# Seven block products for eight in a gated MLP

## The chip, the cores and the metric

The kernel runs on one core of a Trainium2 chip. A core has TensorE (PE; matmuls, with the load of the stationary operand shown apart as PEld), VectorE (DVE), ScalarE (ACT), GpSimd (POOL) and SyncE (SP, which issues DMAs here). The metric is device time in microseconds for one execution: the median of three runs.

## The reference

A decoder block over 1024 tokens of width 1024 in float32: a gated-DeltaNet branch and a latent-attention branch, merged by gates and added to the input, then the gated MLP with a causal depthwise convolution of three taps, and a final norm. The change concerns the MLP:

```python
h = rmsnorm(x, norm_ffn_g[l])
u = causal_dwconv(jnp.einsum("bsd,df->bsf", h, w_up[l]), conv_ffn_w[l])
gate_f, up_f = u[..., :D_FF], u[..., D_FF:]
x = x + jnp.einsum("bsf,fd->bsd", jax.nn.silu(gate_f) * up_f, w_down[l])
...
return rmsnorm(x, norm_final_g)
```

D_FF is 2816, that is 22 tiles of 128 features; `w_up` has 2 x 2816 columns (gate and up).

## The kernel before

Every float32 operand of a large product is cut in two fp32r parts, `hi` (a cast on ScalarE) and `lo` (value minus `hi`, on VectorE). A product of two operands is then three matmuls, lo x hi, hi x hi and hi x lo, of 128 x 128 by 128 x 512 into one PSUM bank (`mm3` at L372, `proj_step` at L388).

The parts up to the merge of the branches take the first 1260 us and are not touched. After them `tail` (L1524) projects the merged rows with `w_out`, one token tile at a time (`out_proj`, L1486): the input rows are added (L1506), squared (L1508), scaled by the norm's root and gain (L1512); then TensorE transposes the rows to features (`transpose_rows`, L1514; L1519), and ScalarE and VectorE cut them into `h2` (L1521, L1522). The weights of `out_proj`'s left side are cut at L1494 and L1495. The eight rows of x, 4 MB, stay in SBUF for the rest of the kernel.

`ffn` (L1554) goes over 22 feature tiles. `up(ft)` makes two products, one for gate and one for up: 8 rows of weights x 2 token halves x 3 matmuls each. Each product fills two banks. ScalarE starts the convolution out of PSUM (L1574), VectorE does the other two taps (L1577), ScalarE the silu (L1580), GpSimd the product of gate and up (L1584; the last tile's on VectorE), and the activation is cut at L1585 and L1586. Weights come in through `load_w` (L349; the cuts are L355 and L356). After every two tiles `down` multiplies the two activations of the tiles before with their rows of `w_down` for 8 token tiles x 2 halves (L1600, matmuls at L375 to L377), and VectorE adds each bank to x (L1601). The last four tiles' down-products are interleaved with the final norm (L1629 to L1655). The activations never leave SBUF.

The order of the instructions on each engine is that of the program in `tail` and `ffn`; in the last part, and in all parts before the merge, it is written out by a planner (`Flow`, L170): threads yield instructions with an estimated time, and the most urgent that is ready goes first. Its times are constants such as `0.07 + 0.00104 * n` us for VectorE (L138). On the chip each engine takes its queue in that order and waits on semaphores where data is not ready.

Of the kernel before, what the change touches and what calls it, by code (L numbers as in the profile page):

```python
# [8 lines left out]
F32 = mybir.dt.float32  # L9
# [60 lines left out]
class Memory:  # L70
    """SBUF in KB per partition: regions of one type at a time, and in them the places of tiles, by name."""
# [57 lines left out]
def mm(n, fn):  # L129
    """A float32 product with n columns."""  # L130
    return "pe", 0.0017 * n, fn, None
# [18 lines left out]
def sp(us, fn):  # L150
    """A load that takes the memory for this time."""
# [110 lines left out]
class Block:  # L262
# [27 lines left out]
    def small_constants(self, flow):  # L290
        """Matrices and per-channel vectors; rows of 128 channels turn into columns on the tensor engine."""
# [38 lines left out]
    def bank(self, tag, *shape):  # L330
        """The next PSUM tile of a ring; two banks for "mm"."""
# [17 lines left out]
    def load_w(self, src, kt, n, keep=None):  # L349
        """Streams a weight block [P, kt, n] and splits it exactly into two fp32r parts."""  # L350
# [11 lines left out]
    def rstd(self, ss, n, name):  # L362
        """(ss / n + eps) ** -0.5 for a small [P, m] tile."""
# [24 lines left out]
    def proj_step(self, ps, w, r, k, n):  # L388
        """The k-th of the n terms of a product in two banks."""
# [10 lines left out]
    def mix_in(self, flow, hT):  # L400
# [9 lines left out]
        def mean_root(ss, n, name):  # L410
            """(ss / n + eps) ** -0.5."""
# [141 lines left out]
    def decays(self, flow, ab):  # L553
        """Per-token log decay (softplus without overflow or cancellation), its sums in a chunk, beta."""
# [55 lines left out]
    def load_steps(self, flow, n, src):  # L610
        """Weights of job n: their load, then their split into two parts."""
# [15 lines left out]
    def gdn_conv(self, ps, n, out=None, acc=None):  # L627
        """Of one head's projected q, k or v by feature: causal convolution over time, silu."""
# [13 lines left out]
    def gdn_decay(self, flow, h, pre):  # L642
        """Decays from one token of a chunk to a later one, as exponentials of sums; zero to an earlier one."""
# [21 lines left out]
    def gdn_prepare(self, flow, h, kq, pre):  # L665
        """Key norms and score matrices of every chunk, values by token."""
# [75 lines left out]
    def gdn_blocks(self, flow, h, ma):  # L742
        """Inverses of the diagonal blocks of I + M by forward substitution, half of a block's columns per partition, on M^T's blocks."""
# [37 lines left out]
    def gdn_inverse(self, flow, h, ma, pre):  # L781
        """Transposed inverse of the unit lower triangle I + M of every chunk: pairs of blocks merge,
# [938 lines left out]
```

## Time and profile before

| | |
|---|---|
| median of three runs | 2082.28 us (2081.77 to 2082.43) |
| span of the profiled execution, first to last instruction | 2080.7 us |
| TensorE busy | 2064.0 us, 99% |
| VectorE busy | 1200.3 us, 58% |
| ScalarE busy | 790.0 us, 38% |
| GpSimd busy | 245.8 us, 12% |
| DMA | 142.13 MB, mean 68 GB/s |
| MLP | from 1350 us to the end |

The profile is of one execution; its span lies 1.6 us under the median of the runs, the work around the first and last instruction. Busy time of TensorE includes pipelined matmuls that overlap, so the mean length of one matmul (395 ns) is not its price; the distance from one to the next is. Busy shares are averages over all stages.

### The profile page before, as it was taken

The numbers are of one execution on the slowest core, as the hardware profiler recorded it, in microseconds if no ns is written. First come the engines' busy times: TensorE is split into PE (matmuls) and PEld (weight loads), VectorE is DVE, ScalarE is ACT, GpSimd is POOL, SyncE is SP. The second block draws the span as 40 slices with busy tenths as digits, with TensorE's granted clock in tenths as the row PEclk, the third lists the DMA queues.
The fourth block names the chain that finished last, engine by engine and source line by source line (L and its number), as shares of the span: only waits on it lengthen the run. The fifth ranks groups of instructions, "written<-read, shape, count | busy, mean of one in ns | idle before, by whom it ended". The sixth has DMA issues, their size and how long they took to land.

```text
span 2080.7 us, 27905 instructions
## 1 busy us (share of the span) xinstructions
PE 2064.0 (99%) x11037; PEld 1730.2 (83%) x11037; DVE 1200.3 (58%) x2355; ACT 790.0 (38%) x1698; POOL 245.8 (12%) x230
## 2 busy tenths in 40 slices
PE   9999999999999999999999999999999999999998
PEld 8987888888888888888888888888888888888887
DVE  7377678778788635666674223345354543445436
ACT  5275365366354435554462112232221222222223
POOL 3132021022020002020000031001000000000000
PEclk9999999999999999999999999999999999999999
DMA  6122212212212341111127343012111111111112
GB/s 209 46 60 64 77 39 63 68 48 54 77 49 54 107 133 31 32 37 34 46 90 225 121 134 110 1 56 67 51 51 41 49 53 51 51 38 47 58 31 82
DMA packets 183896, 142.13 MB, mean 68 GB/s; under 512 B 42410, under 2 KB 165012, under 8 KB 183764
## 3 DMA queue, kind: packets, MB, share of 16 engines
q1 hardware_dynamic: 174756, 120.60, 19.9%
q10 hardware_dynamic: 7056, 12.65, 1.7%
q0 software_dynamic: 1952, 7.08, 1.0%
q8 instruction: 87, 1.43, 0.3%
q14 instruction: 45, 0.37, 0.1%
HBM read 114.36 MB, written 25.95 MB: 67 GB/s over the span
## 4 chain that ended last, share of the span: by engine, by line
PE 95%; DVE 2%; DMA 1%; ACT 1%; issue 0%; SPq 0%; POOLq 0%; POOL 0%; ACTq 0%
PE psum L392 54%; PE psum L375 6%; PE psum L377 6%; PE psum L376 6%; PE psum L1395 5%; PE psum L490 3%; PE psum L1404 3%; PE psum L1349 1%; PE psum L1501 1%; PE psum L1504 1%; PE psum L1503 1%; PE psum L680 1%; PE psum L872 1%; PE psum L906 1%; PE psum L916 1%; PE psum L874 1%
## 5 line engine op out<-in xcount | busy, mean ns | idle before, releaser
L392 PE MATMUL psum<-ht,w 128*128 128x512 f32 x4800 | 1171.0, 395 | 1.0 <-ACT ht L1418 0.7
L392 PEld LDWEIGHTS psum<-ht,w 128*128 128x128 f32 x4800 | 881.7, 188 | 172.7 <-ACT ht L1418 1.3
L1577 DVE SCALAR_TENSOR_TENSOR s<-psum,cols,s 128x1023 f32<-128x1023 f32 x88 | 112.6, 1279 | 234.5 <-ACT s L1574 234.5
L1574 ACT ACTIVATE s<-psum,cols 128x1024 f32<-128x1024 f32 x44 | 49.1, 1117 | 212.4 <-PE psum L392 212.4
L375 PE MATMUL psum<-s,s 128*128 128x512 f32 x320 | 124.5, 389 | 0.0
L376 PE MATMUL psum<-s,s 128*128 128x512 f32 x320 | 124.5, 389 | 0.0
L377 PE MATMUL psum<-s,s 128*128 128x512 f32 x320 | 124.5, 389 | 0.0
L1584 POOL TENSOR_TENSOR s<-s 128x1024 f32<-128x1024 f32 x21 | 50.3, 2396 | 611.5 <-DVE s L1577 611.5
L637 DVE SCALAR_TENSOR_TENSOR s<-psum,cols,s 128x511 f32<-128x511 f32 (+1 forms) x144 | 105.2, 739 | 5.0 <-ACT s L632 4.8
L767 DVE TENSOR_TENSOR s<-sc,s 64x240 f32<-64x240 f32 (+27 forms) x248 | 85.3, 344 | 5.3 <-DMA sc<-md_dram 0.7
L769 DVE TENSOR_TENSOR s<-s 64x240 f32<-64x240 f32 (+27 forms) x248 | 80.9, 326 | 6.0
L1601 DVE TENSOR_TENSOR s<-s,psum 128x512 f32<-128x512 f32 x72 | 49.5, 687 | 48.2 <-PE psum L377 48.2
L1329 DVE TENSOR_REDUCE nm<-psum 128x1 f32<-128x256 f32 (+5 forms) x64 | 48.3, 756 | 41.6 <-PE psum L1396 41.6
L624 DVE TENSOR_TENSOR w<-raw,w 128x512 fp32r<-128x512 f32 x96 | 65.5, 686 | 10.5 <-ACT w L622 10.4
L376 PEld LDWEIGHTS psum<-s,s 128*128 128x128 f32 x320 | 60.1, 188 | 12.5
L377 PEld LDWEIGHTS psum<-s,s 128*128 128x128 f32 x320 | 60.1, 188 | 12.5
L375 PEld LDWEIGHTS psum<-s,s 128*128 128x128 f32 x320 | 60.1, 188 | 12.4
L355 ACT CAST s<-raw 128x1024 fp32r<-128x1024 f32 x20 | 21.0, 1051 | 129.8 <-PE psum L376 116.7
L392 PE MATMUL psum<-s,w 128*128 128x512 f32 x288 | 69.8, 391 | 0.0
L490 PE MATMUL psum<-s,ht 128*128 128x400 f32 (+1 forms) x384 | 69.7, 336 | 0.0
L1395 PE MATMUL psum<-ht 128*128 128x384 f32 (+5 forms) x288 | 65.0, 352 | 0.1
L1585 ACT CAST s<-s 128x1024 fp32r<-128x1024 f32 x22 | 23.1, 1051 | 110.4 <-POOL s L1584 106.4
(377 smaller groups left out, 3332.1 us busy)
## 6 DMA issues: line engine op xcount, KB each, us to landing
raw<-in_w_in_dram SPq DMA_DIRECT2D x48, 512.0 KB, 4.5
raw<-in_w_up_dram SPq DMA_DIRECT2D x23, 512.0 KB, 3.9
rx<-in_w_up_dram SPq DMA_DIRECT2D x21, 512.0 KB, 3.9
raw<-in_w_down_dram SPq DMA_DIRECT2D x21, 512.0 KB, 3.6
sg_dram<-s ACTq DMA_DIRECT2D x16, 512.0 KB, 2.7
s<-sg_dram SPq DMA_DIRECT2D x16, 512.0 KB, 3.6
s<-in_x_dram SPq DMA_DIRECT2D x12, 512.0 KB, 6.2
oa_dram<-s POOLq DMA_DIRECT2D x8, 512.0 KB, 3.1
```

The costliest lines, as they stand in the source:

```text
L375: self.nc.tensor.matmul(ps, lhsT=ll, rhs=rh, start=first, stop=False)
L376: self.nc.tensor.matmul(ps, lhsT=lh, rhs=rh, start=False, stop=False)
L377: self.nc.tensor.matmul(ps, lhsT=lh, rhs=rl, start=False, stop=last)
L392: product = lambda o, l, r, **kw: pe(0.2155, lambda: self.nc.tensor.matmul(o, lhsT=l[:, k, :], rhs=r, **kw))
L490: yield pe(0.000417 * (b - a), lambda: tensor.matmul(ps[:, u, :b - a], lhsT=l[:, k, cs], rhs=w[:, k, a:b], start=n == 0, stop=n == 3 * KD ...
L624: yield dve(512, lambda: nc.vector.tensor_tensor(out=lo[:, c], in0=raw[:, c], in1=f(hi[:, c]), op=ALU.subtract))
L637: yield dve(570, lambda: nc.vector.scalar_tensor_tensor(out=o, in0=src[:, max(a - d, 0):b - d], scalar=self.cw[:, n, j:j + 1], in1=o, op0= ...
L767: yield dve(n * w, lambda: nc.vector.tensor_tensor(out=t, in0=mb[:, j, j + 1:].unsqueeze(2).to_broadcast(sh), in1=xb[:, j, :w].unsqueeze(1 ...
L769: yield dve(n * w, lambda: nc.vector.tensor_tensor(out=xb[:, j + 1:, :w], in0=xb[:, j + 1:, :w], in1=t, op=ALU.subtract))
L1395: nc.tensor.matmul(ps[:, n, :w], lhsT=l, rhs=r[:, n * w:(n + 1) * w], start=t == 0, stop=t == len(terms) - 1 and n != parts - 1)
L1404: self.nc.tensor.matmul(po[:, q0:], lhsT=x[:, j, :], rhs=y[:, j, q0:], start=x is vl and j == 0, stop=y is ptl and j == b)
L1577: nc.vector.scalar_tensor_tensor(out=acc[:, d:], in0=src[:, :S - d], scalar=self.cf[:, n, j:j + 1], in1=acc[:, d:], op0=ALU.mult, op1=ALU.add)
```

## The change

Both products of the MLP are done by Strassen's scheme in Winograd's form. An operand is a 2 x 2 matrix of blocks; seven products p1 to p7 of blocks and of sums of blocks take the place of eight, and the sums cost additions on the other engines.

Up: the 2 x 2 blocks are gate and up columns against two halves of the 8 weight rows, and the two token halves. The token side's sums are made once, in `rows_out`, out of the transposed rows (t1 to t4); the rows of x go to DRAM as soon as they are known. The weight side's four sums of each tile are made by GpSimd (`sums`). A pair of gate and up tile then uses four PSUM banks; p1 is copied to a second bank (`seed`), p7 to SBUF (`copy`), and two additions on PSUM (`third`, `fourth`) combine partial results in the middle of the matmuls. The convolution, silu and gate product are as before, but the activation goes to DRAM.

Down: a stage of its own after all 22 tiles. It takes the tiles in three groups of 2m (m = 3, 4, 4). Blocks of activations (L) and of `w_down` (R) are read from DRAM; GpSimd makes four sums of L blocks and VectorE four of R blocks; ScalarE and VectorE cut the operands of each product; the products go to PSUM banks 0 to 3 and 4 to 7 in turns, one more copy (`seed`) shares p1, and VectorE adds banks into the reloaded x. The projection, the up stage and the down stage are all in one plan of `Flow`, so that stages overlap where places in SBUF come free.

```diff
-    def mm3(self, ps, l, r, first, last):
-        nc = self.nc
+    def mm3(self, ps, l, r, first, last, **kw):
         (lh, ll), (rh, rl) = l, r
-        self.nc.tensor.matmul(ps, lhsT=ll, rhs=rh, start=first, stop=False)
-        self.nc.tensor.matmul(ps, lhsT=lh, rhs=rh, start=False, stop=False)
-        self.nc.tensor.matmul(ps, lhsT=lh, rhs=rl, start=False, stop=last)
+        self.nc.tensor.matmul(ps, lhsT=ll, rhs=rh, start=first, stop=False, **kw)
+        self.nc.tensor.matmul(ps, lhsT=lh, rhs=rh, start=False, stop=False, **kw)
+        self.nc.tensor.matmul(ps, lhsT=lh, rhs=rl, start=False, stop=last, **kw)
...
+        def row(s, b, ps):
...
+            yield dve(1150, lambda: vector.tensor_tensor(out=t, in0=y, in1=t, op=ALU.add))
+            ss = self.rowstat[:, s, 0:1]
+            yield act(1150, lambda: scalar.activation(out=y, in_=t, func=AF.Square, accum_out=ss))
...
+            r = yield from self.mean_root(s, D)
...
+            yield dma(lambda: nc.sync.dma_start(out=self.x2_dram[s], in_=t))
+            yield LOAD
+            flow.give("x", x)
+            flow.post(("stored", s))
+            if s == order[-1]:
+                flow.give("wraw", 3)
+            if all(("stored", n) in flow.when for n in range(NS)):
+                flow.give("sums", 0)
...
+        def turned(j):
+            c, c2 = slice(j * P, (j + 1) * P), slice(512 + j * P, 512 + (j + 1) * P)
+            if j:
+                yield On(("first sum", j - 1), ("sums", j - 1), ("h", j - 1))
+            p11 = yield from turn(j, 0, 3)
...
+            flow.post(("left", j))
+            p12 = yield from turn(j + 4, 0, 4)
...
+            yield act(512, lambda: scalar.copy(out=t1, in_=p12))
+            flow.post(("turned", j))
+            yield sub(t3, p22, t1)
+            yield sub(t1, t1, p11)
+            flow.post(("first sum", j))
+            flow.fork(halves_of("t1", t1, c, j), 0.8)
+            yield sub(t2, p22, t1)
+            yield sub(t4, p21, t2)
+            flow.post(("sums", j))
+            yield from halves("h", p22, c)
+            flow.post(("h", j))
...
+        def rest(name, half, at):
+            (hi,), (lo,) = h2[name]
+            yield On("projected")
+            for j in range(4):
...
+                c, src = slice(j * P, j * P + P), mg[half][:, :, at + j * P:at + j * P + P]
+                yield act(512, lambda: scalar.copy(out=hi[:, :, c], in_=src))
...
+        def sums():
+            for ft in range(NF):
...
+                yield Get("sums")
+                g, u = raws[ft, 0][1], raws[ft, 1][1]
+                t = self.m("sums", P, 4, 4, P)
+                lo, hi = slice(0, 4), slice(4, 8)
+                for n, x, y, op in ((0, u[:, lo], u[:, hi], ALU.add), (1, t[:, 0], g[:, lo], ALU.subtract),
+                                    (2, g[:, lo], u[:, lo], ALU.subtract), (3, g[:, hi], t[:, 1], ALU.subtract)):
+                    yield pool(1.2, lambda: nc.gpsimd.tensor_tensor(out=t[:, n], in0=x, in1=y, op=op))
+                raws[ft] = t
+                flow.post(("wsums", ft))
...
+                x = yield Get("wop")
+                both = self.m(f"wop{x}", P, 2, 4, P, dt=F32R)
+                hi, lo = both[:, 0], both[:, 1]
+                yield act(512, lambda: scalar.copy(out=hi, in_=src))
+                yield dve(512, lambda: vector.tensor_tensor(out=lo, in0=src, in1=f(hi), op=ALU.subtract))
...
+                if name == "p3":
+                    flow.give("sums", 0)
+                    for part in range(2):
+                        flow.give("wraw", raws[ft, part][0])
...
+        def pair(ft):
+            a = 4 * (ft % 2)
+            c, d, e = a + 1, a + 2, a + 3
...
+            free = {0: {"a": ["projected", ("h", 2), ("op", 3)], "e": [("first sum", 3)], "d": []},
+                    1: {"a": [("turned", 3), ("op", 7)], "e": [("sums", 3)], "d": ["marked"]}}.get(ft, dict(a=[("evicted", ft - 2)], e=[], d=[]))
+            yield On(*free["a"])
+            def seed():
+                yield act(540, lambda: scalar.copy(out=bank(c), in_=bank(a)))
+                flow.post(("seed", ft))
+            def add(out, event):
+                yield On(("copied", ft), *free["d"])
+                yield dve(620, lambda: vector.tensor_tensor(out=bank(out), in0=bank(c), in1=p7, op=ALU.add))
+                flow.post((event, ft))
...
+            def copy():
+                yield On(("operand", "t1"), ("operand", "t2"))
+                yield act(540, lambda: scalar.copy(out=p7, in_=bank(e)))
+                flow.post(("copied", ft))
...
+            yield from term(ft, "p1", a, True)
+            flow.fork(seed(), 2)
+            if ft < 2:
+                yield On(("seed", ft))
+                yield from term(ft, "p2", a, False)
+            for name in ("p6", "p7") if ft < 2 else ("p7", "p6"):
+                if name == "p7":
+                    yield On(*free["e"])
+                    yield from term(ft, "p7", e, True)
+                    p7 = self.m("p7", P, 512)
+                    flow.fork(copy(), 2)
+                else:
+                    yield On(("seed", ft))
+                    yield from term(ft, "p6", c, False)
+                    flow.post(("summed", ft))
+            flow.fork(add(d, "third"), 2)
+            if ft > 1:
+                yield On(("seed", ft))
+                yield from term(ft, "p2", a, False)
+            yield On(("third", ft))
+            yield from term(ft, "p5", c, False)
+            flow.fork(add(e, "fourth"), 2)
+            yield from term(ft, "p4", d, False)
+            yield On(("fourth", ft))
+            yield from term(ft, "p3", c, False)
+            flow.fork(evict(ft, a), 3)
+        def evict(ft, a):
...
-            nc.scalar.activation(out=us[0], in_=us[0], func=AF.Silu)
-            ah = self.m("a_hi", P, S, dt=F32R)
-            al = self.m("a_lo", P, S, dt=F32R)
-            eng = nc.vector if ft == NF - 1 else nc.gpsimd
-            eng.tensor_tensor(out=us[0], in0=us[0], in1=us[1], op=ALU.mult)
...
+        nc, i = self.nc, self.i
+        tensor, scalar, vector = nc.tensor, nc.scalar, nc.vector
+        places = dict(blk={n: at for n, at in enumerate((194, 0, 186, 114, 98, 146, 154, 162, 170, 178, 12, 20))},
+                      lop=dict(enumerate((66, 34))), rop=dict(enumerate((50, 82))))
...
+        groups, f0 = [], 0
+        for m in (3, 4, 4):
+            groups.append((f0, f0 + m, m))
...
+        def free():
+            yield On(("acts", 1))
+            flow.give("blk", 0)
+            last_ft = NF - 1
+            yield On(("w", last_ft, "p3"))
...
+            flow.give("blk", 9)
+            yield On(("fourth", last_ft))
+            flow.give("blk", 2)
...
+            yield On(("p5", last_ft))
+            self.m.open(F32, "sb")
...
+            yield On(("p3", last_ft))
+            self.m.open(F32, "s2", "s3", "w", "s1", "sc", "sd")
+            for n in (5, 6, 10, 11):
+                flow.give("blk", n)
+            flow.post("x2 places")
+            yield On(("acts", last_ft))
...
+        def loads():
+            for n, (fa, fb, m) in enumerate(groups):
+                for name in ("L11", "R11", "L12", "R21", "L21", "L22", "R12", "R22"):
+                    x, t = yield from block(n)
+                    row, col = int(name[1]) - 1, int(name[2]) - 1
+                    f1 = (fa, fb)[col if name[0] == "L" else row]
...
+        def combine(n, side):
...
+                else:
+                    step = dve(512 * m, lambda: vector.tensor_tensor(out=o, in0=a, in1=b, op=kind))
+                yield step
+                blocks[n, to] = out
...
+                s1 = yield from block(n)
+                yield from op(s1, blk("L21"), blk("L22"), ALU.add, "S1")
+                yield On(("cut", n, "L11"))
+                yield from op(blk("L21"), blk("L11"), blk("L21"), ALU.subtract, "S3")
+                yield from op(blk("L11"), s1, blk("L11"), ALU.subtract, "S2")
+                yield On(("cut", n, "L12"))
+                yield from op(blk("L12"), blk("L12"), blk("S2"), ALU.subtract, "S4")
+            else:
+                yield On(("block", n, "R12"), ("block", n, "R22"))
+                t3 = yield from block(n)
+                yield from op(t3, blk("R22"), blk("R12"), ALU.subtract, "T3")
+                yield On(("cut", n, "R11"))
+                yield from op(blk("R12"), blk("R12"), blk("R11"), ALU.subtract, "T1")
+                yield from op(blk("R11"), blk("R22"), blk("T1"), ALU.subtract, "T2")
+                yield On(("cut", n, "R21"))
+                yield from op(blk("R21"), blk("R21"), blk("T2"), ALU.subtract, "T4")
+        factors = dict(p1=("L11", "R11"), p2=("L12", "R21"), p6=("S2", "T2"), p7=("S3", "T3"), p5=("S1", "T1"), p4=("L22", "T4"), p3=("S4", "R22"))
...
+        def cuts(side):
+            for n, (_, _, m) in enumerate(groups):
+                for p in order:
+                    name = factors[p][side]
+                    x = yield Get(("lop", "rop")[side])
+                    both = self.m(f"{('lop', 'rop')[side]}{x}", P, 2, 4, 512, dt=F32R)
+                    yield On(("block", n, name))
...
+                    for k0 in range(0, m, 2):
+                        ks = slice(k0, min(k0 + 2, m))
+                        w = 512 * (ks.stop - ks.start)
+                        yield act(w, lambda: scalar.copy(out=both[:, 0, ks], in_=src[:, ks]))
+                        yield dve(w, lambda: vector.tensor_tensor(out=both[:, 1, ks], in0=src[:, ks], in1=f(both[:, 0, ks]), op=ALU.subtract))
+                    ops[n, p, side] = x, both
...
+        def products():
+            for n, (_, _, m) in enumerate(groups):
+                for p in order:
+                    yield On(("op", n, p, 0), ("op", n, p, 1))
+                    (xl, l), (xr, r) = (ops.pop((n, p, side)) for side in range(2))
+                    base = 4 if p in ("p6", "p5", "p3") else 0
+                    before = dict(p1=("p4", n - 1), p2=("seed", n), p6=("seed", n), p7=("p2", n), p5=("p6", n), p4=("p7", n), p3=("p5", n))[p]
+                    for j in range(4):
+                        if p == "p1" and n == 0:
...
+                            for k in range(m):
+                                cs = slice(j * P, (j + 1) * P)
+                                self.mm3(ps, (l[:, 0, k, cs], l[:, 1, k, cs]), (r[:, 0, k], r[:, 1, k]), p in ("p1", "p7") and k == 0, k == m - 1,
+                                         skip_group_check=p not in ("p1", "p7"))
...
+                        if p == "p1":
+                            flow.fork(seed(n, j), 2)
+                        else:
+                            flow.fork(add(n, p, j), 2)
+                    flow.give("lop", xl)
+                    flow.give("rop", xr)
...
+        def seed(n, j):
+            yield On(("used", "p3", n - 1, j) if n else ("evicted", NF - 1))
+            yield act(540, lambda: scalar.copy(out=self.psum[:, 4 + j, :], in_=self.psum[:, j, :]))
...
+        def add(n, p, j):
+            s, half, base = dict(p2=(j, 0, 0), p6=(j + 4, 0, 4), p7=(j + 4, 1, 0), p5=(j + 4, 1, 4), p4=(j + 4, 0, 0), p3=(j, 1, 4))[p]
+            yield On(("x2", s))
+            o = x2[s][:, halves[half]]
+            yield dve(600, lambda: vector.tensor_tensor(out=o, in0=o, in1=self.psum[:, base + j, :], op=ALU.add))
+            flow.post(("used", p, n, j))
```

The token tiles are projected in the order 0, 4, 1, 5, 2, 6, 3, 7. In the up stage `order` is p1, p7, p6, p2, p5, p4, p3 from the third tile on.

## Rows read from the trace of the kernel before

**Rows 1.** The page of the profile, its head: span, engines' busy time, instructions

```profile
span 2080.7 us, 27905 instructions
...
PE 2064.0 (99%) x11037; PEld 1730.2 (83%) x11037; DVE 1200.3 (58%) x2355; ACT 790.0 (38%) x1698; POOL 245.8 (12%) x230
...
```

**Rows 2.** The chain of waits, 1240 us to the end: start, length, engine, line

```profile
...
1464.09 43.52 PE psum L392 x192
...
2073.14 0.24 PE psum L377
...
```

**Rows 3.** Busy time by window; PE, PEld, DVE, ACT, POOL, clock, DMA, GB/s

```profile
...
1464.09:1529.37 65.28, 65.28 (x289) 54.07 (x289) 30.26 (x32) 14.53 (x15) 4.79 (x2) 1.00 0.16 49
...
```

**Rows 4.** Who waited for whom, TensorE, 1354 us to the end

```profile
...
PE psum L1519 <- DVE s L1512: 0.5, 1, 0.5
```

**Rows 5.** Groups by line and shape, 1230 us to the end

```profile
...
L1577 DVE SCALAR_TENSOR_TENSOR s<-psum,cols,s 128x1023 f32<-128x1023 f32 x44 | 56.5, 1283 | 234.5 <-ACT s L1574 234.5
...
L1584 POOL TENSOR_TENSOR s<-s 128x1024 f32<-128x1024 f32 x21 | 50.3, 2396 | 611.5 <-DVE s L1577 611.5
L1601 DVE TENSOR_TENSOR s<-s,psum 128x512 f32<-128x512 f32 x72 | 49.5, 687 | 48.2 <-PE psum L377 48.2
...
L356 DVE TENSOR_TENSOR w<-rx,w 128x1024 fp32r<-128x1024 f32 x23 | 28.0, 1216 | 0.0
...
L355 ACT CAST s<-raw 128x1024 fp32r<-128x1024 f32 x20 | 21.0, 1051 | 129.8 <-PE psum L376 116.7 <-DMA raw<-in_w_down_dram 13.1
...
L1495 DVE TENSOR_TENSOR w<-s,w 128x512 fp32r<-128x512 f32 x16 | 11.0, 688 | 18.9 <-ACT w L1494 18.9
L1494 ACT CAST w<-s 128x512 fp32r<-128x512 f32 x16 | 9.9, 621 | 68.6 <-PE psum L1504 55.7 <-POOL s L1484 8.5 <-PE psum L392 4.4
...
L1521 ACT CAST ht<-psum 128x512 fp32r<-128x512 f32 x16 | 9.3, 583 | 6.2 <-PE psum L1519 5.9
...
```

**Rows 6.** Timelines of GpSimd and VectorE in two places: start, length

```profile
...
1446.73 2.40 POOL L1584 TENSOR_TENSOR s<-s 128x1024 f32<-128x1024 f32 x1 [18.84 <-DVE s L1577]
1447.10 1.40 DVE L1601 TENSOR_TENSOR sd<-sd,psum 128x512 f32<-128x512 f32 x2
1448.41 1.81 DVE L356 TENSOR_TENSOR w<-raw,w 128x1024 fp32r<-128x1024 f32 x1
...
1968.97 2.40 POOL L1584 TENSOR_TENSOR s<-s 128x1024 f32<-128x1024 f32 x1 [18.83 <-DVE s L1577]
1970.65 1.80 DVE L356 TENSOR_TENSOR w<-raw,w 128x1024 fp32r<-128x1024 f32 x1
...
```

**Rows 7.** The chain of waits after the last projection product, 1349 to 1356 us

```profile
...
1349.60 0.24 PE psum L1504
...
1354.42 0.66 PE psum L1519 x4
...
```

**Rows 8.** Timeline of TensorE at the start of the kernel

```profile
...
7.54 1.27 PE L469 MATMUL psum<-ident,sc 128*128 128x128 f32 x8 [0.70 <-issue]
11.54 1.09 PE L469 MATMUL psum<-ident,sd 128*128 128x128 f32 x4 [2.72 <-ACT ht L473]
...
```

**Rows 9.** Windows of 1 us: length, TensorE busy, granted clock, DMA, GB/s

```profile
...
10.00:11.00 1.00, 0.00 (x0) 0.64 1.04 415
11.00:12.00 1.00, 0.46 (x3) 0.50 1.04 415
...
16.00:17.00 1.00, 1.00 (x5) 0.50 1.02 406
17.00:18.00 1.00, 1.00 (x8) 0.95 1.03 394
...
```

**Rows 10.** DMA issues on the page: size, us from issue to landing

```profile
...
raw<-in_w_up_dram SPq DMA_DIRECT2D x23, 512.0 KB, 3.9
...
raw<-in_w_down_dram SPq DMA_DIRECT2D x21, 512.0 KB, 3.6
sg_dram<-s ACTq DMA_DIRECT2D x16, 512.0 KB, 2.7
...
```

More of the change, by code (lines that the diff above doesn't have):

```diff
@@ L1548, in tail @@
[L1548 to L1565 removed]
+        self.back(mg, w_out, gb)
@@ new lines, in mean_root, with back @@
+    def mean_root(self, s, n):
+        nc = self.nc
+        ss, ms, r = (self.rowstat[:, s, k:k + 1] for k in (0, 2, 3))
+        yield dve(1, lambda: nc.vector.tensor_scalar(out=ms, in0=ss, scalar1=1.0 / n, scalar2=EPS, op0=ALU.mult, op1=ALU.add))
+        yield pool(0.47, lambda: nc.gpsimd.tensor_tensor(out=r, in0=ms, in1=self.mhalf[:, :1], op=ALU.pow))
+        return r
+    def back(self, mg, w_out, gain):
+        for names in (dict(x0=178, x1=182), dict(wraw0=0, wraw1=4, wraw2=8, wraw3=28), dict(sums=178, p7=ring(186, 2, 2)),
+                      {f"wop{n}": at for n, at in enumerate((12, 16, 20, 24, 130, 134, 138, 142))},
+                      {f"u{n}": 162 + 4 * n for n in range(4)}, dict(mh0=20, mh1=22, ml0=24, ml1=26)):
+            self.m.place(**names)
+        self.rowstat = self.small.tile([P, NS, 4], F32, name="rowstat", bufs=1)
+        self.x2_dram = self.dram.tile([NS, P, D], F32, name="x2_dram")
+        self.act_dram = self.dram.tile([NF, P, S], F32, name="act_dram")
+        flow = Flow(op=(1, 5), x=(0, 1), wraw=(0, 1, 2), wop=(0, 1), sums=(), u=(), blk=(), lop=(), rop=())
+        with self.tc.manual_schedule(engines=self.engines):
+            h2 = self.rows_out(flow, mg, w_out, gain)
+            self.ffn_up(flow, h2)
+            self.ffn_down(flow)
+            flow.run()
@@ L1595, in down @@
-        def down(group):
-            ws = {ft: self.load_w_down(ft) for ft in group}
-            for s in range(NS):
-                for ns in halves:
-                    ps = self.bank("dn")
-                    add_product(ps, s, ns, ws, group, True, True)
-                    nc.vector.tensor_tensor(out=x2[s][:, ns], in0=x2[s][:, ns], in1=ps, op=ALU.add)
-        for n, group in enumerate(groups):
-            for ft in group:
-                up(ft)
-            if 0 < n < len(groups) - 1:
-                down(groups[n - 1])
@@ new lines, in mark, with emit, pairs @@
+        def mark():
+            yield On(("h", 3))
+            def emit():
+                for n in range(4):
+                    tensor.matmul(self.psum[:, 6, n * P:(n + 1) * P], lhsT=self.identb, rhs=self.identb, start=n == 0, stop=True,
+                                  skip_group_check=True)
+            yield pe(0.24, emit)
+            flow.post("marked")
+        def pairs():
+            for ft in range(NF):
+                flow.fork(pair(ft), 10 + ft)
+            yield 0.0
+        for steps, rank in ((loads(), 4), (sums(), 4), (splits(), 4), (mark(), 1), (pairs(), 0)):
+            flow.fork(steps, rank)
@@ L1655, in scaled, with sides, finishes @@
             flow.post(("out", s, n))
-        def tiles():
-            for s in range(NS):
-                flow.fork(tile(s), s)
-            yield 8.5
-            flow.post("acts")
-        with self.tc.manual_schedule(engines=self.engines):
-            flow.fork(tiles(), 0)
-            flow.run()
-    def load_w_down(self, ft):
-        hi, lo = (self.m(n, P, 1, D, dt=F32R) for n in ("dhi", "dlo"))
-        return self.load_w(self.i["w_down"][0, ft * P:(ft + 1) * P, :].unsqueeze(1), 1, D, keep=(hi, lo))
+        def sides():
+            for n in range(len(groups)):
+                for side in "LR":
+                    flow.fork(combine(n, side), 5 + n)
+            yield 0.0
+        def finishes():
+            yield On(("used", "p7", last, 3))
+            for s in (4, 5, 6, 7, 0, 1, 2, 3):
+                flow.fork(finish(s), 2.5)
+        for steps, rank in ((free(), 0), (residual(), 3), (loads(), 6), (sides(), 0), (cuts(0), 5), (cuts(1), 5), (products(), 50), (finishes(), 0)):
+            flow.fork(steps, rank)
     def run(self):
```

395 lines of the change are left out of this document (284 added, 111 removed).

## The prediction

> **What bounds the kernel now.** I read the page first: TensorE is busy 99% of a span of 2080.7 us, VectorE 58%, ScalarE 38%, GpSimd 12% [rows 1]. A busy TensorE need not be at its pace, so next the chain of waits through the MLP: it is made of L392 (up) and L375 to L377 (down) alone, and a stretch of 192 up-products takes 43.52 us, 0.2267 us each [rows 2]. The windows view of one period, two up-tiles and one down-group, gives 192 + 96 = 288 products in 65.28 us, 0.2267 us again, with TensorE never idle and VectorE busy 30.26 of it [rows 3]. So both kinds of product have one price, and nothing else is on the path. The list of waits confirms it: from 1354 us to the end TensorE waited once, for 0.5 us [rows 4]. Whatever takes products away saves 0.2267 us each, as long as the other engines still deliver in time; every new wait of TensorE is paid in full, because there is no slack in it now.
>
> **Removed.** Up: 22 tiles x 2 parts x 8 rows of weights x 2 halves x 3 products = 2112. Down: 22 x 16 x 3 = 1056. After: up 22 x 7 blocks x 4 x 3 = 1848; down 7 blocks x 4 x 3 x (3+4+4) = 924. 396 products fewer, x 0.2267 = **89.8 us**. The 64 transposes stay; four small products of `mark` (0.24 us by the planner's entry) are nothing.
>
> **The load on the other engines, up.** A pair (one up-tile, both parts) is 84 products, 19.04 us. VectorE: 7 weight cuts at 0.69 (L1495), 4 convolution steps at 1.28 (L1577), 2 PSUM additions at 0.69 (nearest row L1601): 11.3 us [rows 5]. GpSimd: the gate product 2.40 and 4 weight sums of half its size at 1.20: 7.2 us [rows 5]. ScalarE has 7 casts of 0.62 and 2 PSUM copies of 0.58 [rows 5] beside what it does today. All fit, so on sums alone the pair is TensorE's. The hand-overs inside it are the new waits: p5 waits for `third` (copy of p7, then an addition), p3 for `fourth`. Each is covered by one block of 12 products, 2.72 us; it needs 0.69 plus two hand-overs of some 0.2 (estimate), so 1.6 us are to spare, more than one convolution step (1.28) in front. I take 0.1 us a pair, **2 us**; the ends are 0 and the slower rival below.
>
> **Down.** A group of m=4 is 336 products, 76.2 us; m=3, 57.1 us; together 209.5. VectorE in m=4: 28 cuts of 1024 at 1.22 (L356), 4 R-sums of 2048 at 2.4 (twice that), 24 additions at 0.69: 60.4 us. GpSimd: 4 L-sums at 4.8 (twice L1584): 19.2. In m=3: 14 cuts at 1.22, 14 at 0.69, 4 sums at 1.83, 24 additions: 50.6; GpSimd 14.4 [rows 5]. VectorE alone fits. But the timeline shows that the two do not run side by side. GpSimd runs 1446.73 to 1449.13; two VectorE additions that read PSUM take their usual 0.69 each meanwhile, and the cut that starts at 1448.41 takes 1.81 instead of 1.22, ending 1.1 after GpSimd. Of nine such cuts in the MLP these are the first and the last [rows 6]; each starts while a GpSimd product runs. So a VectorE instruction with two SBUF inputs waits until GpSimd has finished. By that, cuts and sums (43.9) and GpSimd (19.2) exclude each other, and with the additions (16.5) fill 79.6 us against 76.2; for m=3 50.6 + 14.4 = 65.0 against 57.1. Over all groups 224.2 - 209.5 = 14.7 us is the bound if nothing overlaps, 0 if the additions and VectorE's idle fifth always stand against GpSimd. They do so in part, since VectorE takes its queue in order: **5 us**, a third. The planner that writes the queues has no entry for such a block, so it cannot order around it.
>
> The Trainium skill (SBUF — State Buffer, section SBUF: two separate sides) has this as a rule: VectorE and GpSimd share a pair of ports under an exclusive lock, and a VectorE instruction with two SBUF inputs blocks fully against one of GpSimd. The trace agrees (1.81 against 1.22 us). By it the down groups give back up to 14.7 us; by the sum of each engine's own work, nothing.
>
> **Front: from the output projection to full pace, 9 us.** Today the last row's chain, from the last projection product to its first transposes, takes 4.8 us [rows 7], covered by up-products on the other half. After, all sums of token halves need the last row. Cover: p1, p2 of tile 0 (5.4 us), then of tile 1. For the first two tiles p2 goes into p1's bank and waits for the seed copy (0.58 and two hand-overs): 1.0 us twice. Tile 0's p6 needs weight sums, whose place is free only when the last row is stored: row done at some 6.2 (the 4.8 and its second half, an estimate), store 2.7 [rows 10], four sums 4.8, cast and cut 1.3, hand-overs 0.7: 15.7 us after the projection, 18.5 if each sum waits out one cut of 0.69. TensorE has work to 13.8 (48 products 10.9, two quads of transposes 0.9, the two seed waits). So 1.9 to 4.7, taken 2.8. In both tiles p5 follows p7 directly: copy 0.58, addition 0.69, three hand-overs, 1.9 twice. Tile 1's sums wait for tile 0's p3 cut: 0 to 1, taken 0.5. Sum 9.1; ends 4 (planner fills some) and 15.
>
> **Middle: last pair to first down group, 8 us.** The buffers of p1's operands open at `fourth` of the last tile, 4.5 us before its end (p4 and p3 less 0.95). Four cuts 3.8 plus a first cast 1.05: 0.6 us late. p6 needs R12, R22, loaded only when the last product is done: 768 KB each at 3.6 us per 512 KB [rows 10], landed about 7 us on; then three R-sums 5.5. VectorE also owes the last tile's convolutions 5.1, the cuts of p2 and p6 7.6 and three additions 2.1: 20.3 in all, against p1 and p2's 16.3 us. Late by 4; by 17 if GpSimd's three L-sums and the gate product (13.2) all exclude it. Convolutions and additions (7.2) can run against GpSimd, which leaves 10 at most. Between 4 and 10 I take 7.4, and 0.6 for p1. DMA: 22 activation stores, 8 stores and reloads of x2, the L reads and w_down in blocks, all on SP's queue; transfers of 2.7 to 3.9 us [rows 10] against waits of tens, hidden except where named.
>
> **Clock.** After the gap that ends at 11.54 us [rows 8] the granted clock is 0.64 and then 0.50, back to 0.95 in the window at 17 us [rows 9]: 1.2 GHz for some 6.4 us, 3.2 lost. Gaps of 0.5 us cost nothing [rows 4]. Two stalls above are of that length: **6 us**, between 0 and 13 (four).
>
> The Trainium skill (TensorE: Matmul & The Clock Gate, section Why this matters for your kernels) also warns that idle gaps between bursts of matmuls throttle the clock; the rows show it at the start of this kernel.
>
> **Tail.** Last product to last store as today; VectorE has nothing to cut in the last block: **1 us**, 0 to 3.
>
> **Sum.** 2080.7 - 89.8 + 9 + 2 + 8 + 5 + 6 + 1 = 2021.9 of span. The median, 2082.28, is 1.6 over the span; so 2023.5 us. What this kernel's measurement can tell from no change is 0.2%, about 4 us.
>
> **Rivals.**
> *Nothing is lost beyond some 15 us* (GpSimd stands against additions and idle time, the clock stays up): front and middle at their lower ends and 2 for the rest, 2082.3 - 89.8 + 4 + 4 + 2 = 2002.5; up to 2008 counts here. For it: VectorE alone needs 79% of a group, and waits are covered by whole blocks. Against: rows 6. 0.20.
> *VectorE and GpSimd become the bound of down and its entry*: groups 14.7, middle 17, front 15, clock 13, up 5, tail 3: 68 given back, 2060; anything over 2045 counts here. For it: 79.6 us of VectorE and GpSimd in a group of 76.2, and 65.0 in 57.1. 0.14.
> *Slower: the PSUM additions are on the path in every pair.* Place: `third` and `fourth`, 44 hand-overs. Price: a convolution step 1.28, then a cut with the gate product in front, 0.69 + 2.40, addition 0.69, hand-overs 0.4: 5.5, less 2.72 cover, 2.7 each, 119 us; with the front and middle 2082.3 - 89.8 + 119 + 17 = 2128. It decides from 1.6 us each, (89.8 - 17) / 44. Against: VectorE is busy 11.3 of 19.04 us, and the gate product comes after the convolutions, when `third` is through. 0.03.
> *No gain, the pace per product rising to 0.26*: both kinds run at 0.2267 whatever the operands [rows 2, 3]. 0.01, within 0.2%.
>
> My forecast, 30 us given back, 2008 to 2045: 0.62. The range leaves out half of the best case's lower part and most of the worst: 1999 to 2052. Faster 0.96, same 0.01, slower 0.03.
>
> **What would show it.** 1848 and 924 products of the MLP at 0.2267 us. TensorE idle in pairs 2 to 21 under 3 us in all; some 10 us idle within 40 us after the projection and 8 after the last pair, with a granted clock below 1 behind one or two of them; cuts of 1.22 drawn out to 3 us or more while GpSimd sums; waits of TensorE for VectorE cuts at p6 of each group. I am wrong if pairs take clearly over 19.1 us, if the down groups take their 209.5 us with GpSimd's sums beside VectorE's cuts at full pace, or if the path leaves TensorE for DMA.

## The result and the profile after

The changed kernel takes **2032.18 us** in the median (2030.94 to 2034.51, 4 runs) against 2082.03 (2081.52 to 2082.43, 4 runs) for the kernel before: a ratio of 0.9767 [0.9753, 0.9781]. The forecast was 2023.5 in a range of 1999 to 2052: the sign and the range held, and the forecast was 8.7 us low. Of the 89.8 us removed, 40.4 come back (2031.3 of span against 2080.7), where the sum had 31. They came back in the stages where the prediction looked for them, but not always at the block it named.

The head of the page after, for [rows 1]:

```profile
span 2031.3 us, 27793 instructions
...
PE 1987.2 (98%) x10645; PEld 1660.7 (82%) x10645; DVE 1410.7 (69%) x2504; ACT 896.5 (44%) x1920; POOL 443.4 (22%) x331
...
PE 89%; DVE 6%; DMA 1%; ACT 1%; issue 1%; POOL 0%; SPq 0%; POOLq 0%; ACTq 0%; DVEq 0%
```

TensorE has 392 instructions less: 396 products gone, `mark`'s four added. The last line is the chain that ended last, over the whole span. The same line of the page before:

```profile
PE 95%; DVE 2%; DMA 1%; ACT 1%; issue 0%; SPq 0%; POOLq 0%; POOL 0%; ACTq 0%
```

VectorE's part of the chain has grown from 2% to 6%. Next the windows view of pairs 2 to 21, and of 20 us at the entry of the down stage, in the columns of [rows 3]:

```profile
1398.54:1787.78 389.24, 389.24 (x1717) 322.32 (x1718) 300.19 (x266) 164.37 (x245) 168.29 (x97) 1.00 0.27 86
1790.00:1810.00 20.00, 12.72 (x48) 9.86 (x47) 20.00 (x10) 6.57 (x9) 17.57 (x5) 0.78 0.87 339
```

In the pairs TensorE is busy in every one of 389.24 us, at the full clock. At the entry of the down stage it works 12.72 of 20 us, at 0.78 of its clock, while VectorE is busy throughout with ten instructions and GpSimd for 17.57 with five. The list of TensorE's waits from 1353 us on, for [rows 4] (total, times, longest):

```profile
PE psum L376 <- DVE ht L2013: 12.4, 5, 6.6
PE psum L374 <- ACT ht L2012: 4.0, 2, 3.7
PE psum L374 <- ACT psum L1796: 3.3, 2, 2.6
PE psum L374 <- DVE psum L1801: 2.8, 2, 1.4
PE psum L1637 <- DVE s L1618: 2.0, 1, 2.0
PE psum L374 <- DVE w L1768: 1.4, 1, 1.4
PE psum L374 <- DVE s L1768: 0.4, 1, 0.4
```

L2012 and L2013 are the casts and cuts of the down operands: 16.4 us. The other five rows, 9.9 us, lie in the first two up-tiles. TensorE's timeline says which block each of the longest was in (the wait stands at the end):

```profile
1358.63 0.50 PE L374 MATMUL psum<-ht,w 128*128 128x512 f32 x1 [2.63 <-ACT psum L1796]
1363.48 0.66 PE L1637 MATMUL psum<-ident,s 128*128 128x128 f32 x4 [2.00 <-DVE s L1618]
...
1805.95 0.80 PE L376 MATMUL psum<-ht 128*128 128x512 f32 x1 [6.60 <-DVE ht L2013]
1818.84 0.77 PE L374 MATMUL psum<-ht 128*128 128x512 f32 x1 [3.66 <-ACT ht L2012]
...
1870.56 0.80 PE L376 MATMUL psum<-ht 128*128 128x512 f32 x1 [3.05 <-DVE ht L2013]
```

In order, TensorE waited there for the seed before p2 of tile 0, the scale of row 7, the cut of **p2** of the first group (its third product needs the lower part), the cast of p6, and the cut of p1 of the second group. A smaller wait for a cut, 1.62 us at 1849.10, is in p4 of the first group. What VectorE and GpSimd did around the longest, for [rows 6]:

```profile
1791.98 5.12 DVE L2013 TENSOR_TENSOR ht<-s,ht 128x512 fp32r<-128x512 f32 x2
1797.03 1.27 DVE L1846 SCALAR_TENSOR_TENSOR s<-psum,cols,s 128x1023 f32<-128x1023 f32 x1
1798.22 3.84 DVE L1972 TENSOR_TENSOR w<-w,s 128x1536 f32<-128x1536 f32 x1
1801.98 1.27 DVE L1846 SCALAR_TENSOR_TENSOR s<-psum,cols,s 128x1022 f32<-128x1022 f32 x1
1803.17 2.72 DVE L2013 TENSOR_TENSOR ht<-s,ht 128x512 fp32r<-128x512 f32 x1
...
1792.20 3.83 POOL L1970 TENSOR_TENSOR s<-sb,s 128x1536 f32<-128x1536 f32 x1 [12.38 <-DMA s<-act_dram]
1796.10 4.34 POOL L1970 TENSOR_TENSOR sb<-s,sb 128x1536 f32<-128x1536 f32 x1
1800.52 8.70 POOL L1970 TENSOR_TENSOR s<-s,s 128x1536 f32<-128x1536 f32 x2
```

The first row takes two cuts of different size together. The view of line L2013 from 1790 to 1800 us keeps them apart (shortest, median and longest in ns):

```profile
L2013 DVE TENSOR_TENSOR ht<-s,ht x2: 684/2604/4525, 1792.0 to 1792.6; 128x512 fp32r<-128x512 f32 x1, 128x1024 fp32r<-128x1024 f32 x1
```

While GpSimd sums (L1970), a cut of 1024 columns takes 4.53 us in place of 1.22, a sum 3.84 in place of 1.74 and p2's last cut 2.72 in place of 0.69, 7.4 us of stretching; the cut of 512 that began ahead of GpSimd keeps its 0.68, and the convolution steps (L1846), which read PSUM, keep their 1.27. Last the windows of 1 us, for [rows 9]:

```profile
1367.00:1368.00 1.00, 1.00 (x4) 0.77 (x3) 1.00 (x2) 0.32 (x1) 0.00 (x0) 0.50 0.78 229
...
1807.00:1808.00 1.00, 1.00 (x4) 0.81 (x3) 1.00 (x1) 0.00 (x0) 1.00 (x1) 0.50 0.07 29
1822.00:1823.00 1.00, 1.00 (x4) 0.81 (x3) 1.00 (x2) 0.00 (x0) 0.00 (x0) 0.50 0.41 23
1872.00:1873.00 1.00, 1.00 (x4) 0.80 (x3) 1.00 (x1) 0.33 (x1) 0.00 (x0) 0.50 0.00 0
```

The clock fell four times, each time around one of these waits. Busy time times missing clock, summed over the windows of each fall, is 2.7 (front), 2.8, 2.9 and 2.9 us: 11.3. With the waits, 26.35 from 1353 us on and 1.1 in the projection, that makes 38.8 us, or 38.3 without the 0.5 that TensorE waited there before, of the 40.4; the rest is less than two runs of the kernel differ by.

### The profile page after: what moved, and what is told of

Same layout as the page of the kernel before. It is cut to its first block, busy times and chain, and to the rows that moved or that the text cites. A ratio compares the mean times of both kernels' runs of the same rounds, so it can differ in the third digit from the quotient of the medians.

```text
span 2031.3 us, 27793 instructions
## 1 busy us (share of the span) xinstructions
PE 1987.2 (98%) x10645; PEld 1660.7 (82%) x10645; DVE 1410.7 (69%) x2504; ACT 896.5 (44%) x1920; POOL 443.4 (22%) x331
## 3 DMA queue, kind: packets, MB, share of 16 engines
q8 instruction: 84, 1.38, 0.3%
## 4 chain that ended last, share of the span: by engine, by line
PE 89%; DVE 6%; DMA 1%; ACT 1%; issue 1%; POOL 0%; SPq 0%; POOLq 0%; ACTq 0%; DVEq 0%
PE psum L391 32%; PE psum L374 11%; PE psum L376 11%; PE psum L375 11%; PE psum L1394 5%; PE psum L489 3%; PE psum L1403 3%; DVE ht L2013 2%; PE psum L1348 2%; PE psum L1568 1%; PE psum L1571 1%; PE psum L1570 1%; PE psum L679 1%; PE psum L871 1%; PE psum L905 1%
## 5 line engine op out<-in xcount | busy, mean ns | idle before, releaser
L391 PE MATMUL psum<-ht,w 128*128 128x512 f32 x2688 | 686.9, 400 | 0.7 <-ACT ht L1417 0.4
L391 PEld LDWEIGHTS psum<-ht,w 128*128 128x128 f32 x2688 | 485.0, 188 | 90.4 <-ACT ht L1417 1.1
L1846 DVE SCALAR_TENSOR_TENSOR s<-psum,cols,s 128x1023 f32<-128x1023 f32 x88 | 112.6, 1279 | 59.7 <-ACT s L1843 58.7
L376 PE MATMUL psum<-ht 128*128 128x512 f32 x308 | 123.9, 402 | 12.4 <-DVE ht L2013 12.4
L374 PE MATMUL psum<-ht 128*128 128x512 f32 x308 | 123.2, 400 | 4.1 <-ACT ht L2012 4.0
L375 PE MATMUL psum<-ht 128*128 128x512 f32 x308 | 122.7, 398 | 0.0
L1852 POOL TENSOR_TENSOR s<-s 128x1024 f32<-128x1024 f32 x22 | 54.2, 2463 | 185.7 <-ACT w L1767 96.8
L2012 ACT CAST ht<-s 128x1024 fp32r<-128x1024 f32 (+1 forms) x58 | 54.8, 982 | 63.6 <-PE psum L376 57.6
L376 PEld LDWEIGHTS psum<-ht 128*128 128x128 f32 x308 | 59.7, 194 | 27.5 <-DVE ht L2013 15.1
L2013 DVE TENSOR_TENSOR ht<-s,ht 128x1024 fp32r<-128x1024 f32 (+1 forms) x58 | 80.6, 1409 | 0.0
L1483 POOL TENSOR_TENSOR s<-s 128x1024 f32<-128x1024 f32 x4 | 13.2, 3288 | 286.7 <-DMA rx<-in_w_o_mla_dram 261.5
L374 PEld LDWEIGHTS psum<-ht 128*128 128x128 f32 x308 | 59.9, 195 | 17.6 <-ACT ht L2012 4.8
L374 PE MATMUL psum<-ht,s 128*128 128x512 f32 x184 | 71.7, 390 | 0.4 <-DVE s L1768 0.4
L376 PE MATMUL psum<-ht,s 128*128 128x512 f32 x184 | 71.6, 389 | 0.0
L375 PE MATMUL psum<-ht,s 128*128 128x512 f32 x184 | 71.6, 389 | 0.0
L374 PE MATMUL psum<-ht,w 128*128 128x512 f32 x168 | 66.9, 398 | 4.7 <-ACT psum L1796 3.3
```

The lines of the kernel that those rows point to most:

```text
L391: product = lambda o, l, r, **kw: pe(0.2155, lambda: self.nc.tensor.matmul(o, lhsT=l[:, k, :], rhs=r, **kw))
L1846: yield dve(1160, lambda: vector.scalar_tensor_tensor(out=acc[:, d:], in0=src[:, :S - d], scalar=self.cf[:, n, j:j + 1], in1=acc[:, d:], o ...
L2013: yield dve(w, lambda: vector.tensor_tensor(out=both[:, 1, ks], in0=src[:, ks], in1=f(both[:, 0, ks]), op=ALU.subtract))
```

## Experiments

All ratios are against the kernel before; differences between experiments are between medians. The changed kernel is the base of each edit.

**1. Is it GpSimd's sums?** Two runs. The first leaves out the additions of the L blocks (S1 is set to zero, S3, S2, S4 are summed over 2 of 512 columns), so that GpSimd does little in the first part of the down stage (busy 9.0 of the 93 us from 1787 on); the second moves the sums to VectorE.

```diff
-  step = pool(0.0024 * 512 * m, lambda: nc.gpsimd.tensor_tensor(out=o, in0=a, in1=b, op=kind))
+  step = dve(512 * m, lambda: vector.tensor_tensor(out=o, in0=a, in1=b, op=kind))
```

> Leaves out the additions of the L blocks in the down stage: S1 is a memset by GpSimd, S3, S2 and S4 are summed over 2 of each 512 columns only; the order of all queues is that of the changed kernel. Theory (a VectorE instruction with two SBUF inputs waits for a GpSimd instruction that reads SBUF): cuts and R-sums between 1790 and 1877 us return to 0.69, 1.22 and 1.75 us, TensorE's 16.4 us of waits there fall below 6, and the time to 2008 to 2018 us. Rival (VectorE has too much work of its own there, or loads are late): waits as before, 2029 to 2035 us.

> The L-sums of the down stage on VectorE in place of GpSimd, nothing left out. Theory (blocking): VectorE takes on four sums of 1.75 us in the first group and eight of 2.3 us later, 13.8 us of it by 1877 us, and is no longer stretched, by about 24 us there; waits of TensorE in the down stage fall from 16.4 to some 8 us, the time to 2020 to 2027 us. Rival (VectorE's own work is the limit): more waits, 2035 to 2045 us.

Without the additions 2017.05 us, 0.9685 [0.9669, 0.9702], 15.1 less, and the down stage's waits fall from 16.4 to 6.6 us. Not all that is left is VectorE's own work: beside the last tile's gate product one sum there still takes 3.94 us, and another has waited 2.59 us for a load of `w_down`. On VectorE 2022.62, 0.9714 [0.9699, 0.9728], 9.6 less, though VectorE has 12 more sums to do. The groups by line and shape from 1788 us on show why (count, busy, mean ns). The changed kernel's cuts of 1024:

```profile
L2013 DVE TENSOR_TENSOR ht<-s,ht 128x1024 fp32r<-128x1024 f32 x47 | 70.4, 1512 | 0.0
```

And with the L sums on VectorE, the cuts and two of the sums:

```profile
L2013 DVE TENSOR_TENSOR ht<-s,ht 128x1024 fp32r<-128x1024 f32 x44 | 53.0, 1219 | 0.2 <-ACT ht L2012 0.2
...
L1970 DVE TENSOR_TENSOR s<-s,s 128x1536 f32<-128x1536 f32 x2 | 3.5, 1744 | 0.0
```

The cut is back at 1.22 us, and a sum of 128x1536 that took 3.8 to 4.8 on GpSimd takes 1.74. GpSimd's sums cost more in VectorE's lost time than they save it.

**2. Order of the products.** p7 ahead of p6, so that the third block needs fewer sums.

```diff
-  order = ("p1", "p2", "p6", "p7", "p5", "p4", "p3")
+  order = ("p1", "p2", "p7", "p6", "p5", "p4", "p3")
```

> Order of the down stage's products p1, p2, p7, p6, p5, p4, p3: p7 needs one sum on each side (S3, T3; S1 goes ahead of S3), p6 the end of a chain of three. Theory (the chain of sums behind p6 is what is late): the waits of 6.6 us and 3.1 us in front of that place shrink to under 3 in all and the clock stays up there: 2020 to 2026 us. Rival (VectorE's whole amount of work in the stretch sets the pace, whatever comes first): within 3 us of 2032.

2029.61 us, 0.9751 [0.9737, 0.9766]: 2.6 less, with an interval that overlaps that of the changed kernel, and the waits stay where they were (6.56 in p2, 3.90 at the third block). While GpSimd blocks VectorE, which block comes third makes no difference that these runs can tell.

**3. Is each fall of the clock paid for?** Products on zeros fill the gaps, in two runs; the first has them behind p2 and p6 of group 0 and p2 of group 1, the second as here.

```diff
+            self.nc.vector.tensor_tensor(out=self.strict, in0=f(self.strict), in1=f(self.strict), op=ALU.subtract)
...
+                    idle = {("p1", 0): 29, ("p2", 0): 16, ("p3", 0): 13}.get((p, n), 0)
...
+                        for _ in range(idle):
+                            self.nc.tensor.matmul(ps, lhsT=self.strict, rhs=r[:, 0, 0], start=False, stop=True, skip_group_check=True)
```

> Products with a zero operand (29, 16 and 13 of them) added into a finished bank behind p2 and p6 of the first down group and p2 of the second, where TensorE waits 6.6, 3.7 and 3.1 us; they change no value. Theory (each fall of the granted clock costs what it takes from the products behind it): three falls of 6.4 to 10 us at 1.2 GHz go, 8 us saved, 2024 us. Rival (in the entry the operands set the pace and a faster TensorE only waits longer for the next ones; only the last of the three falls is on the path): 2.7 us saved, 2029 us.

> Products on a weight of zeros fill the three gaps of the down entry where they really are: 29 behind p1 of group 0 (the gap of 6.6 us inside p2), 16 behind p2 (3.66 us before p6), 13 behind p3 of group 0 (3.05 us in p1 of group 1). They add nothing to the sums. Theory A (each fall of the clock is on the path): no half clock at 1801, 1818 and 1870, where 17.9 us of work ran at half rate, so 8.9 us less: about 2023. Theory B (VectorE's work sets when the operands come; a fall ahead of a later wait is free): the first two falls are taken back by longer waits at the next operand, and only the last fall counts: about 2029, with a wait of some 3 us left beside the filling before p6.

The first missed both: 2037.75 us, 0.9791 [0.9777, 0.9806]. The gaps lie a block or two earlier than was taken for it, so of its 13.1 us of products 5.6 came on top of the time. The second, in the right places, gives 2032.90, 0.9766 [0.9753, 0.9780], no difference. TensorE's timeline there:

```profile
1799.35 6.95 PE L2055 MATMUL psum<-ht,strict 128*128 128x512 f32 x29
...
1814.50 3.91 PE L2055 MATMUL psum<-ht,strict 128*128 128x512 f32 x16
1820.96 0.47 PE L374 MATMUL psum<-ht 128*128 128x512 f32 x1 [2.55 <-ACT ht L2013]
...
1852.34 0.50 PE L376 MATMUL psum<-ht 128*128 128x512 f32 x1 [3.26 <-DVE ht L2014]
```

The fall at 1801 is gone and p2 runs at full rate, but p6 comes when VectorE lets it: behind 3.91 us of filling TensorE waits 2.55 more, where 3.66 in all had been enough. The wait of 1.62 in p4 of the first group becomes 3.26, with a fall of its own. The missing clock of the down stage shrinks from 8.6 to 3.4 us (two falls of 1.7), and the time doesn't move. So the mechanism of theory B holds, and its number doesn't: the fall at 1869 is gone as well, but the 3 us that it was to bring are not in the time. In this part of the down stage VectorE set the time, and half-rate products only filled it.

**4. Order or amount of VectorE's work?** With the L sums on VectorE, its queue puts cuts ahead of sums; then p7 ahead of p6 as well.

```diff
-  flow.fork(combine(n, side), 5 + n)
+  flow.fork(combine(n, side), 7 + n)
```

> As the run with the L sums on VectorE (2022.62 us), and in VectorE's queue the cuts of operands stand ahead of the sums of blocks; nothing left out. Theory A (order: p2's cut is late only because two sums stand ahead of it, 5.65 us): the wait of 5.48 us before p2 goes and with it a fall of the clock, about 2014 to 2017. Theory B (amount: convolutions, sums, cuts and additions that VectorE owes before p6 are 23.5 us against some 17 of products): the wait moves to p6 at about its size: 2021 to 2023.

> As the run before it (L sums on VectorE, cuts ahead of sums), and p7 ahead of p6 in each group, so that only three sums in place of five stand before the third block; nothing left out. Theory B (amount of VectorE's work before the third block): 23.5 less two sums is 20 us, and the third block is late by 2 to 3 us only, with one or no fall of the clock: 2013 to 2017, 5 us or more below the run before it. Theory A (order alone): as the run before it, within 2 us.

2018.28 us, 0.9697 [0.9684, 0.9711], and 2014.16, 0.9678 [0.9665, 0.9691]. In the first the wait in p2 goes and one of 6.35 us opens at p6, as theory B says; but the time falls by 4.3, between the two, since one long wait and one fall remain where there were two of each. In the second, theory B's case, the longest wait of the down stage is 1.53 us, and the clock stays up:

```profile
1788.00:1896.00 108.00, 101.94 (x443) 82.21 (x442) 103.86 (x100) 45.39 (x56) 5.54 (x1) 1.00 0.62 221
```

The order of products, which showed nothing in experiment 2, is worth 4.1 us here, once VectorE isn't blocked by the sums: more than the 2 of theory A, short of the 5 that theory B asked for.

**5. The front.** Two edits apart: the seeds of tiles 0 and 1 ahead of the casts in ScalarE's queue, and their weight sums on VectorE.

```diff
-            flow.fork(seed(), 2)
+            flow.fork(seed(), 0 if ft < 2 else 2)
```
```diff
-                    yield pool(1.2, lambda: nc.gpsimd.tensor_tensor(out=t[:, n], in0=x, in1=y, op=op))
+                    if ft < 2:
+                        yield dve(512, lambda: vector.tensor_tensor(out=t[:, n], in0=x, in1=y, op=op))
+                    else:
+                        yield pool(1.2, lambda: nc.gpsimd.tensor_tensor(out=t[:, n], in0=x, in1=y, op=op))
```

> For tiles 0 and 1 the seed copy is set ahead of the casts of the token sums in ScalarE's queue; nothing else moves. Theory (the seed's place in the queue is what TensorE pays for): the wait of 2.63 us before tile 0's p2 falls to about 1 us (0.58 us of copy and two hand-overs), so 1.6 us less, and up to 3 more if the clock then no longer falls there: 2027.5 to 2030.6. Rival (the wait only hides a later one, the scale of row 7 that ends 2.00 us late): the later waits grow by what this one loses, 2032 as for the changed kernel.

> The sums of weight blocks of tiles 0 and 1 are made on VectorE in place of GpSimd; nothing left out, everything else as in the changed kernel. Theory (in the front too VectorE stands behind GpSimd: three instructions of row 7 took 1.77, 1.76 and 1.75 us in place of 0.69): the waits of 2.00 and 1.38 us for row 7's scale and for the weight cut fall by some 3 us together, and the clock may stay up there for 2 to 3 more: 2026 to 2029.5. Rival (the four sums of 0.69 now stand in VectorE's own queue, which has no idle time from 1353 to 1370, and are late there instead): 2031 to 2035.

The seed alone: 2031.72 us, 0.9760 [0.9746, 0.9773], no difference. Its wait falls from 2.63 to 1.09, and the next ones grow (1.76 and 1.61 for row 7's scale, 1.85 for the weight cut): the rival. The sums alone: 2027.56, 0.9739 [0.9726, 0.9752], 4.6 less, the theory. VectorE's timeline in the changed kernel, at row 7:

```profile
1358.30 1.77 DVE L1618 SCALAR_TENSOR_TENSOR s<-s,rowstat,gc 128x512 f32<-128x512 f32 x1
1359.99 1.76 DVE L1698 TENSOR_TENSOR s<-s,s 128x512 fp32r<-128x512 f32 x1
1361.68 1.75 DVE L1618 SCALAR_TENSOR_TENSOR s<-s,rowstat,gc 128x512 f32<-128x512 f32 x1
```

And with the front's sums on VectorE:

```profile
1359.47 0.75 DVE L1618 SCALAR_TENSOR_TENSOR s<-s,rowstat,gc 128x512 f32<-128x512 f32 x1
1360.14 0.69 DVE L1698 TENSOR_TENSOR s<-s,s 128x512 fp32r<-128x512 f32 x1
1360.74 0.75 DVE L1618 SCALAR_TENSOR_TENSOR s<-s,rowstat,gc 128x512 f32<-128x512 f32 x1
```

Counted from the first product of tile 0's p2 (1358.63 and 1359.81 us), row 7 is 3.1 us earlier, and its waits and the fall of the clock behind them are gone. Part comes back as a wait of 2.34 us for a weight cut of tile 0, so the waits of the front shrink only from 9.9 to 8.6; 2.7 more are the clock's. That is 4.0 us for the front, and from the projection's wait near 1270 us to p5 of tile 1 the trace is 4.1 us shorter. The planner also ordered the down stage anew: its waits sum to 16.6 us, much as before, but 7.82 of them now stand before p2, for the down stage's seed copy, and its missing clock is 4.6 instead of 8.6. So the 4.6 us of the median agree with the front's 4, but this run doesn't show that they are the front's alone.

**6. Together.** L sums on VectorE, cuts first, p7 ahead of p6, front sums on VectorE; then the seeds too.

> L sums on VectorE, cuts ahead of sums, p7 ahead of p6 (the run of 2014.16 us), and the weight sums of tiles 0 and 1 on VectorE as well; nothing left out. If the front is worth what the theory of the run before it says: 2008 to 2011.5. If not: 2013 to 2017.

> As the run before it, with the seed copies of tiles 0 and 1 ahead of the casts in ScalarE's queue. Where row 7's scale no longer waits for GpSimd, the 1.6 us of the seed can show: 1.5 us below the run before it. Rival: another instruction of row 7 is late instead, no difference within 1 us.

2010.65 us (2007.20 to 2011.31, 5 runs), 0.9655 [0.9642, 0.9668], and 2009.57 (2007.85 to 2010.66, 4 runs), 0.9652 [0.9639, 0.9665]. Both beat the kernel before by 3.5% and the changed kernel by some 22 us. The front's 3.5 us is what it was alone, within the spread: over the stretch of the trace from the projection's wait to p5 of tile 1 it is 3.7 us here and was 4.1 alone. The seeds make no difference that these runs can tell. The first of the two still waits here:

```profile
PE psum L374 <- ACT psum L2058: 4.1, 1, 4.1
PE psum L374 <- ACT psum L1799: 3.4, 2, 2.6
PE psum L374 <- DVE psum L1804: 2.9, 2, 1.5
PE psum L374 <- DVE s L1771: 2.3, 1, 2.3
```

The largest is now for the down stage's seed copy (L2058). In ScalarE's queue it stands behind a cast that waited 6.49 us for a sum on VectorE, and that sum stands in VectorE's queue among the last tile's convolutions.

## Why the prediction was right, and where not

- **Removed**, right: 1848 and 924 products, 0.2267 us each wherever TensorE doesn't wait.
- **Up pairs** (2 us), right: 0 in twenty pairs. The slower rival is dead: `third` cost 1.41 us in each of tiles 0 and 1, where p5 follows p7 directly; `fourth`, which p4 covers, cost nothing there, and neither did anything from tile 2 on. The prediction said 1.9 for `third`; 1.41 less a copy of 0.58 and an addition of 0.69 leaves 0.14 for all three hand-overs, which it had put at some 0.2 each.
- **Front** (9), right in size (9.9) by luck, since its parts were not: the seed waits were 2.63 and 0.71 instead of 1.0 twice, the first for the casts that stand ahead on ScalarE; p6's weight sums, priced at 2.8 by their own length, held TensorE up for 0.4 only, and cost most by holding VectorE up on row 7 (waits of 2.00 and 1.38 that the prediction had not). The rule applied to the down stage holds in the front too, and the prediction didn't apply it there.
- **Middle** (8), undersized and put one block too late. It costed p6 from loads and sums. But p2's last cut stood behind a sum in VectorE's queue, and was 6.6 us late; the stretching of that sum, of a cut ahead of it and of itself is 7.4 us. With p6's 3.66 and small ones, 11.7. The prediction had named the total blocking as its far end and taken a middle value; the first experiment puts the price of the blocking at 15 us over the whole down stage.
- **Groups** (5), right in size (4.7), not in place: 1.62 in p4 of the first group and 3.05 in p1 of the second. The waits at p6 of each group, named as a sign, came in the first group alone; from p2 of the second group on TensorE doesn't wait at all, although GpSimd sums there too. The share of a third was a guess that came out.
- **Clock** (6), mis-sized and wrongly a term of its own: four falls instead of two, 11.3 us of missing clock, of which 8.6 in the down stage were not to be had apart from VectorE's lateness (experiment 3). The front's 2.7 were saved in experiment 5, together with the gaps that made them.
- **Tail** (1): 7.2 us behind the last product, as before: 0. A wait of 1.1 us for a cut of the projection's weights at 1270 us was not foreseen.

So the mechanism was right, and the forecast was too low by the two terms that it under-sized, the clock (5.3 us) and the middle (3.7); the pairs and the tail, which cost nothing, took back 3 of these 9.

By the rule of the Trainium skill (SBUF — State Buffer, section SBUF: two separate sides) whichever of VectorE and GpSimd starts first holds the ports for its whole instruction and the other fully blocks, if VectorE has two SBUF inputs and GpSimd reads SBUF. The trace agrees: the cut of 512 that starts at 1791.98, ahead of GpSimd's start at 1792.20, takes its 0.68 us, and the cut of 1024 behind it ends at 1797.10, 1.1 us after GpSimd's end at 1796.03; and the instructions that read PSUM aren't stretched.

## What to carry to other kernels

Before you give GpSimd elementwise work, look at what VectorE does meanwhile: where it is the fuller engine and reads SBUF twice, a sum of 1.74 us on VectorE is cheaper than one of 4 us beside it. When an engine in order is late, ask first how much it owes by then and then in which order: with GpSimd's sums out of the way, cuts first was worth 4.3 us and p7 first 4.1, and p7 first before that nothing that could be told (cuts first was not tried before that). Filling a gap to keep the clock up was worth nothing where the operands behind it came from the engine that made the gap; no run here shows a case where it pays.

## What the hardware showed that was not expected

GpSimd is stretched as well as VectorE. Of its eight sums of 2048 columns three took 4.56 to 4.63 us and five 5.46 to 5.53. The first four sums, of 1536, took 3.83, 4.34, 4.82 and 3.80, where three quarters of 4.56 would be 3.42 (an estimate). What each took beyond that, 0.4, 0.9, 1.4 and 0.4, is within 0.2 us the time for which a VectorE instruction still ran after the sum had started (0.5, 1.0, 1.5, 0.5). With the sums on VectorE, one of them still took 3.90 us in place of 1.74, beside the last tile's gate product, which the kernel before had on VectorE and the changed one has on GpSimd. And the length of a gap alone didn't decide the clock: in the front the wait of 2.63 us left it at its full level (1.00 in every window of 1 us from 1358 to 1364), and the next, of 2.00 us, was followed by 0.70 in the window at 1364 and by half the level, 0.50, from 1365 on. With the front's sums on VectorE waits of 2.63 and 2.34 us stand 13 us apart, and it stays at 1.00.
